# A float32 streaming-encoder block on one core: the down projection as seven block products, with weight sums formed by adding transfers

## The chip, the cores and the metric

The kernel runs on one core of one Trainium2 chip. A core has a matrix engine (TensorE, called PE in the profile, with its weight loads as PEld), three engines for elementwise work (VectorE or DVE, ScalarE or ACT, GpSimd or POOL), a queue engine that here only issues transfers (SyncE or SP), and 16 DMA engines that carry the transfers issued by SP, ACT and POOL. The engines run at the same time; each takes its own instructions in order, and an instruction waits for semaphores that others raise. The metric is the device time of one execution in microseconds; less is better.

## What is computed

One layer: 512 tokens of 1024 features, with 16 learned tokens put in front, go through two attention branches, a merge, a gated feed-forward part with a short convolution, and residual norms. All of it is float32. The change touches only the last product, the down projection, and what leads to it:

```python
hn = _rmsnorm(h, norm_ffn_pre[l])
up = hn @ w_ffn_up[l]
act = jax.nn.gelu(_causal_dwconv(up, conv_w[l], conv_b[l]), approximate=True)
ffn = (act * (hn @ w_ffn_gate[l])) @ w_ffn_down[l]
h = h + _rmsnorm(ffn, norm_ffn_post[l])
```

`w_ffn_down` is 2816 by 1024, and 512 tokens of the result are returned. So the last line multiplies a 512 by 2816 matrix with a 2816 by 1024 one, scales each token by its root mean square and a gain, and adds `h`.

## The kernel before, in words

**Products in three parts.** TensorE multiplies in a short format here (float32r). To keep float32 accuracy, each operand x is split into a high part, a copy cast to float32r, and a low part, x minus the high part. A product is the sum of three: high by high, high by low, low by high. A split is two instructions on two engines: a cast on ACT (line 88 in `load_w`, line 134 in `split`), and then a subtraction that reads the cast (line 89, on POOL for weights; line 135, on DVE for activations).

**The feed-forward loop** (lines 919 to 942) runs over `FT` = 22 blocks of 128 features. For each block `m` it loads 128 columns of the up and of the gate weights, multiplies them with the normed tokens (`pt_up`, 48 matmuls; `ga`, 24 matmuls), applies the convolution and GELU to the first product, multiplies the two, and splits the result into `fh` and `fl`, which stay in SBUF. The normed tokens are `h2h` and `h2l`; the residual `hb` stays in SBUF to the end.

**The down projection** (lines 945 to 1006) is in three column ranges. Columns 0 to 511: for each of 11 chunks of weights (two blocks of 128 rows by 512 columns, 512 KB) it loads, splits, and runs 24 matmuls of 512 columns, for four tiles of 128 tokens (`d01`, `d23`). Columns 512 to 767: six chunks, matmuls of 256 columns (`dq`). Columns 768 to 1023: all weights are loaded and split first (`raw_e`, `wdh`, `wdl`), then one token tile after the other is multiplied (`e`), so that the norm, the residual and the store of a tile run while the next tile is multiplied. In all this stage, 22 blocks by 4 token tiles by 3 products give 264 matmuls for each column range.

**What sets the order.** The program is written as above, and a scheduler places the instructions on each engine; within an engine the order is then fixed. SP carries all weight loads in one queue. Three `raw` buffers of 512 KB are shared by all weight loads, so a load waits until an earlier chunk has been split. The split chunks have two buffers in the pool `wp` (tags `wh`, `wl`).

Of the kernel before, what the change touches and what calls it, by code (L numbers as in the profile page):

```python
# [49 lines left out]
def block_kernel(ctx: ExitStack, tc: tile.TileContext, x, meta_tokens, norm_mix_pre, w_in, w_gk_up, b_gk,  # L50
# [155 lines left out]
    def diagonal(pl, r, n, nm):  # L206
        """r on the diagonal: a product with it transposes and scales by token."""
        d = pl.tile([P, P], F32, tag="dr", name=f"dr{nm}", bufs=2)
        dve.tensor_scalar(out=d[:n, :n], in0=ident[:n, :n], scalar1=r, scalar2=None, op0=ALU.mult)
        return d[:n, :n]  # L210

    with tc.tile_pool(name="p0", bufs=2, side="right") as p0:
        xts = {i: p0.tile([P, D], F32, name=f"xt{i}", bufs=1) for i in range(1, 5)}
# [115 lines left out]
    # =================== gated linear attention ===================  # L329
    with ExitStack() as pgs:  # L330
        pgc = pgs.enter_context(tc.tile_pool(name="pgc", bufs=1))
        # masks: level masks by compressed query, and the diagonal
# [248 lines left out]
    with tc.tile_pool(name="pa", bufs=1) as pa:  # L581

        def sb_parts(j, k, q, v):
            """Both parts of a head's keys stacked, against each part of its queries twice; values with both parts side by side."""
# [66 lines left out]
        def sb(j, ks, qh, ql, vs):  # L651
# [115 lines left out]
    # the last two meta tokens: too few for the array, their products are summed over the blocks of 128 rows first  # L767
# [36 lines left out]
    with tc.tile_pool(name="pw", bufs=1) as pw:  # L804
# [7 lines left out]
        def gained(i, pt, hf):  # L812
            """Half of the mixed output of a tile with the gain, and its sum of squares."""
# [12 lines left out]
        def normed(i):  # L826
            """Residual, second norm, and both parts of the result by feature."""
# [16 lines left out]
        def mini():  # L844
            """The same for the last two meta tokens, by feature from the start."""
# [30 lines left out]
        # the first half of the columns for all tokens, then the second one token tile at a time  # L876
# [38 lines left out]
        normed(4)  # L915
    p2.close()

    # =================== gated MLP with the causal convolution ===================
    pq = ctx.enter_context(tc.tile_pool(name="pq", bufs=1, side="right"))
    fh = pq.tile([P, FT, SEQ], F32R, name="fh")  # L920
    fl = pq.tile([P, FT, SEQ], F32R, name="fl")
    with tc.tile_pool(name="pu", bufs=2) as pu:
        for m in range(FT):
            pt = proj(load_w(cols(w_up, m * P), KT, f"up{m}", into=wx if m % 2 else None), h2h, h2l, FFNS, f"up{m}", apart=m < 2)
            y = pu.tile([P, SEQ], F32, tag="y", name=f"cy{m}")
# [14 lines left out]
            dve.tensor_tensor(out=y, in0=pg_, in1=y, op=ALU.mult)  # L940
            split(fh[:, m, :], fl[:, m, :], y)
# [4 lines left out]
    # =================== down projection, norm, residual ===================  # L946
    with tc.tile_pool(name="pd", bufs=1) as pd:
        QC = 256
        wdh = pd.tile([P, FT, QC], F32R, name="wdh")
        wdl = pd.tile([P, FT, QC], F32R, name="wdl")  # L950
        pos = [mmt("d01"), mmt("d23")]
        p4 = [pst(f"dq{i}", "sz"[i % 2]) for i in range(4)]
        ssq = pd.tile([P, 4, 3], F32, name="ssq")

        def down(c0, ncol, dsts):
            step = 1024 // ncol
            for k0 in range(0, FT, step):
                nk = min(step, FT - k0)
                wh, wl = load_w(w_down[k0 * P : (k0 + nk) * P, c0 : c0 + ncol].rearrange("(k p) m -> p k m", p=P), nk, f"d{c0}_{k0}")
                for kk in range(nk):  # L960
                    k = k0 + kk
                    for i in range(4):
                        t = slice(i * P, i * P + P)
                        for q, (a, b) in enumerate(((fh, wh), (fh, wl), (fl, wh))):
                            pe.matmul(dsts[i], a[:, k, t], b[:, kk, :], start=k == 0 and q == 0, stop=k == FT - 1 and q == 2)  # L965
# [3 lines left out]
        junk = pd.tile([P, 512], F32, name="dj")
        yb = pd.tile([P, 4, D], F32, name="yb")  # L970

        def gain3(i, src, c0):
            n = src.shape[-1]
            dve.tensor_tensor(out=yb[:, i, c0 : c0 + n], in0=src, in1=g3bc[:, c0 : c0 + n], op=ALU.mult)  # L974

        def square(i, src, q):
            act.activation(junk[:, : src.shape[-1]], src, AF.Square, accum_out=ssq[:, i, q : q + 1])  # L977
# [54 lines left out]
```

## Time and profile before

| | us |
|---|---|
| median of 3 runs (981.71 to 983.47) | 981.96 |
| span of the profiled execution | 983.2 |
| TensorE busy in it | 958.5 (97%) |
| down projection, three column ranges on TensorE | 61.60, 31.23, 31.25 |
| from the end of the last matmul (976.92) to the end of the span | 6.28 |

The span is the time from the first to the last instruction of one execution under the profiler; that execution lies 1.2 us above the median of the runs. The median is the number that a change is measured by. TensorE's granted clock is 0.990 over the span.

The page's first part gives the busy time of each engine, its second part the same in 40 slices of 24.6 us. The chain of waits leads back from the last instruction to whatever released each step. A table of windows gives the busy time of each engine in chosen stretches, with the share of the 16 DMA engines in use and the bytes they moved. The groups by line give a mean time for each kind of instruction. A busy TensorE is not by itself a bound; whether anything on it waits is read from the chain and from the idle time before its groups.

### The profile page before, as it was taken

How to read it: one execution, taken by the hardware profiler on the slowest of the kernel's cores; microseconds unless marked ns; L12 is line 12 of the kernel's file. 1: busy time of each engine (PE TensorE's matmuls, PEld its weight loads, DVE VectorE, ACT ScalarE, POOL GpSimd, SP SyncE). 2: the span in 40 equal slices, each digit the busy share in tenths (PEclk: the TensorE clock that was granted, in tenths of full speed). 3: DMA queues.
4: the chain of work that ended last, by engine and by line, in shares of the span. 5: the costliest groups of instructions: out<-in, count | busy, mean ns of one | idle time of the engine just before them, and what ended most of it. 6: DMA issues, size and time to landing. Idle time of an engine off the chain costs nothing.

```text
span 983.2 us, 17022 instructions
## 1 busy us (share of the span) xinstructions
PE 958.5 (97%) x6918; PEld 895.8 (91%) x6918; DVE 558.8 (57%) x970; ACT 461.5 (47%) x868; POOL 401.2 (41%) x285
## 2 busy tenths in 40 slices
PE   7999999999999998999999899999999999999997
PEld 7999999999999998999998779999988999888997
DVE  6675867767547786787849957444343444300112
ACT  5664645545467574676663244533333333311331
POOL 5523232222244454454545433543443443243460
PEclk9999999999999999999999899999999999999999
DMA  7122221222222222222223441333323323223231
GB/s 212 45 65 65 65 55 54 65 66 60 67 58 72 71 65 65 65 65 66 72 58 112 153 144 43 100 95 91 103 86 92 102 86 95 78 86 102 82 117 65
DMA packets 127552, 81.28 MB, mean 83 GB/s; under 512 B 3680, under 2 KB 120162, under 8 KB 127474
## 3 DMA queue, kind: packets, MB, share of 16 engines
q1 hardware_dynamic: 126082, 76.00, 27.0%
q10 hardware_dynamic: 1392, 4.19, 1.1%
q8 instruction: 54, 0.88, 0.4%
q14 instruction: 24, 0.20, 0.1%
HBM read 78.09 MB, written 2.10 MB: 82 GB/s over the span
## 4 chain that ended last, share of the span: by engine, by line
PE 85%; DVE 8%; issue 2%; ACT 2%; POOL 1%; DMA 1%; SPq 1%; DVEq 0%; POOLq 0%; ACTq 0%
PE pt_up L109 13%; PE ga L938 12%; PE d L965 6%; PE pt_gr L109 5%; PE pt_gv L109 5%; PE pt_go L109 4%; PE pt_mg L109 4%; PE e L998 3%; PE dq L965 3%; PE pt_gk L109 2%; PE pt_sv L109 2%; PE wo L887 2%; PE pt_ms L109 2%; PE pt_gq L109 2%; PE pt_sk L109 2%
## 5 line engine op out<-in xcount | busy, mean ns | idle before, releaser
L89 POOL TENSOR_TENSOR wl_up<-raw_up,wh_up 128x1024 fp32r<-128x1024 f32 x22 | 52.9, 2406 | 70.8 <-ACT wh_up L88 70.8
L89 POOL TENSOR_TENSOR wl_ga<-raw_ga,wh_ga 128x1024 fp32r<-128x1024 f32 x22 | 52.6, 2393 | 56.6 <-ACT wh_ga L88 56.6
L929 DVE SCALAR_TENSOR_TENSOR cy<-pt_up,cw,cy 128x511 f32<-128x511 f32 (+1 forms) x44 | 32.8, 746 | 74.1 <-ACT cy L926 74.1
L109 PE MATMUL pt_up<-h2l,wh_up 128*128 128x256 f32 (+1 forms) x352 | 73.6, 283 | 0.3 <-DVE h2l L204 0.2
L109 PE MATMUL pt_up<-h2h,wh_up 128*128 128x256 f32 (+1 forms) x352 | 73.5, 283 | 0.0
L109 PE MATMUL pt_up<-h2h,wl_up 128*128 128x256 f32 (+1 forms) x352 | 73.3, 282 | 0.0
L938 PE MATMUL ga<-h2l,wh_ga 128*128 128x512 f32 (+1 forms) x192 | 72.2, 376 | 0.0
L938 PE MATMUL ga<-h2h,wl_ga 128*128 128x512 f32 (+1 forms) x192 | 72.1, 375 | 0.0
L938 PE MATMUL ga<-h2h,wh_ga 128*128 128x512 f32 (+1 forms) x192 | 72.1, 376 | 0.0
L89 POOL TENSOR_TENSOR wl_d<-raw_d,wh_d 128x1024 fp32r<-128x1024 f32 (+1 forms) x17 | 39.6, 2332 | 63.7 <-ACT wh_d L88 63.7
L88 ACT CAST wh_up<-raw_up 128x1024 fp32r<-128x1024 f32 x22 | 23.0, 1050 | 85.6 <-PE pt_up L109 76.2
L135 DVE TENSOR_TENSOR fl<-cy,fh 128x512 fp32r<-128x512 f32 x22 | 50.2, 2282 | 15.1 <-ACT fh L134 15.1
L109 PEld LDWEIGHTS pt_up<-h2h,wh_up 128*128 128x128 f32 x352 | 56.9, 189 | 1.7
L109 PEld LDWEIGHTS pt_up<-h2l,wh_up 128*128 128x128 f32 x352 | 55.5, 189 | 0.7 <-DVE h2l L204 0.7
L109 PEld LDWEIGHTS pt_up<-h2h,wl_up 128*128 128x128 f32 x352 | 55.4, 189 | 0.0
L88 ACT CAST wh_d<-raw_d 128x1024 fp32r<-128x1024 f32 (+1 forms) x17 | 17.5, 1029 | 65.8 <-PE d L965 45.1
L940 DVE TENSOR_TENSOR cy<-ga,cy 128x512 f32<-128x512 f32 x22 | 15.2, 691 | 49.0 <-PE ga L938 47.9
L938 PEld LDWEIGHTS ga<-h2h,wl_ga 128*128 128x128 f32 x192 | 36.2, 188 | 7.0
L938 PEld LDWEIGHTS ga<-h2l,wh_ga 128*128 128x128 f32 x192 | 36.2, 188 | 6.2
L938 PEld LDWEIGHTS ga<-h2h,wh_ga 128*128 128x128 f32 x192 | 36.2, 188 | 6.1
L974 DVE TENSOR_TENSOR yb<-d,g3bc 128x512 f32<-128x512 f32 x4 | 2.8, 692 | 61.3 <-ACT dj L977 61.2
L965 PE MATMUL d<-wl_d,fh 128*128 128x512 f32 x88 | 34.8, 396 | 0.0
(522 smaller groups left out, 3234.4 us busy)
## 6 DMA issues: line engine op xcount, KB each, us to landing
raw_up<-in_w_ffn_up_dram SPq DMA_DIRECT2D x22, 512.0 KB, 4.0
raw_ga<-in_w_ffn_gate_dram SPq DMA_DIRECT2D x22, 512.0 KB, 3.9
raw_d<-in_w_ffn_down_dram SPq DMA_DIRECT2D x16, 512.0 KB, 3.5
raw_gv<-in_w_in_dram SPq DMA_DIRECT2D x8, 512.0 KB, 3.9
raw_gr<-in_w_in_dram SPq DMA_DIRECT2D x8, 512.0 KB, 3.8
raw_mg<-in_w_in_dram SPq DMA_DIRECT2D x8, 512.0 KB, 3.9
raw_go<-in_w_gla_out_dram SPq DMA_DIRECT2D x8, 512.0 KB, 4.1
raw_ms<-in_w_in_dram SPq DMA_DIRECT2D x8, 512.0 KB, 3.9
```

Of the source, the lines that this page charges most:

```text
L88: act.copy(hi_out, raw)
L89: lo_eng.tensor_tensor(out=lo_out, in0=raw, in1=f32(hi_out), op=ALU.subtract)
L109: pe.matmul(dst, a[:, k, :], b[:, k, lo:hi], start=n == 0, stop=n == len(steps) - 1)
L135: dve.tensor_tensor(out=lo, in0=src, in1=f32(hi), op=ALU.subtract)
L887: pe.matmul(d0[i], m[k][:, t], w, start=k == 0 and q == 0, stop=k == 7 and q == 2)
L929: dve.scalar_tensor_tensor(out=y[:, d:], in0=pt[:, : SEQ - d], scalar=c, in1=y[:, d:], op0=ALU.mult, op1=ALU.add)
L938: pe.matmul(pg_[:, lo:hi], a[:, k, :], b[:, k, lo:hi], start=lo == 0 and k == 0 and q == 0, stop=k == KT - 1 and q == 2, skip_group_check= ...
L940: dve.tensor_tensor(out=y, in0=pg_, in1=y, op=ALU.mult)
L965: pe.matmul(dsts[i], a[:, k, t], b[:, kk, :], start=k == 0 and q == 0, stop=k == FT - 1 and q == 2)
L974: dve.tensor_tensor(out=yb[:, i, c0 : c0 + n], in0=src, in1=g3bc[:, c0 : c0 + n], op=ALU.mult)
L998: pe.matmul(dst, a[:, k, t], b[:, k, :], start=k == 0 and q == 0, stop=k == FT - 1 and q == 2)
```

## The change

The 512 by 2816 by 1024 product is cut into halves three ways: the tokens into two halves of 256, the 1024 columns into `L` and `R`, and the 22 feature blocks into the even (11) and the odd (11) ones. That gives eight block products in the plain way. The changed kernel forms seven (Strassen's scheme in Winograd's form, with signs turned so that the weight sums only add):

- Of the activations it needs four sums besides the blocks `A11`, `A12`, `A22`: `S1`, `S2`, `S3`, `S4`. They are formed on DVE in the feed-forward loop, once for each pair of blocks, on 256 tokens. `A11` and `S1` are split there at once (`Ah`, `Al`); the other five stay whole in `As` and are split again chunk by chunk when their product runs (`sh`, `sl`).
- Of the weights it needs four sums besides the blocks, in the two buffers `tw` and `tv`, 2.9 MB each. T1 (both halves of the even rows) is loaded into `tw` by SP, and the other half is added by transfers issued on POOL with `accum_op=ALU.add`: the transfer reads what lies in SBUF, adds the weights from DRAM, and writes the sum back. T2 adds a third block to `tw` on DVE (line 1035). T4 adds a fourth to `tw` by adding transfers again (line 1079). T3 adds one to `tv` by adding transfers (line 1090).
- The products run in the order p1, p5, p6, p2, p3, p7, p4. Each has 11 blocks by 2 token tiles by 3 products = 66 matmuls of 512 columns. A product's chunk of weights is 512 KB as before; the last chunk has half of that. All splits of weights are now a cast on ACT and a subtraction on DVE; POOL has none in this stage.
- The accumulators are added up on DVE, ACT and in PSUM (p2 runs on top of p1, p3 on top of p5, p7 on top of p6).
- `hb` is written to DRAM before the feed-forward loop (line 919, issued by ACT) and read back into `hbr` (line 1084, issued by SP).

The core of the diff:

```diff
+        for i in range(4):
+            act.dma_start(hbd[i], hb[:, i, :])
...
+            p = m // 2
+            dve.tensor_tensor(out=yp[:, 2, :], in0=yp[:, 1, :], in1=As[:, A22, p, :], op=ALU.subtract)
+            split(Ah[:, :, p, :], Al[:, :, p, :], yp[:, 0:3:2, :])
+            dve.tensor_tensor(out=As[:, S3, p, :], in0=yp[:, 0, :], in1=yp[:, 1, :], op=ALU.subtract)
+            dve.tensor_tensor(out=As[:, S2, p, :], in0=yp[:, 2, :], in1=yp[:, 0, :], op=ALU.subtract)
+            dve.tensor_tensor(out=As[:, S4, p, :], in0=As[:, S2, p, :], in1=As[:, A12, p, :], op=ALU.add)
...
+        def product(nm, operand, source, dsts, first, last):
+            for n, (q, nk) in enumerate(CH):
+                src = source(q, nk)
+                pl_ = pd if turn[0] % 2 else wp
+                turn[0] += 1
+                wh = pl_.tile([P, nk, HC], F32R, tag="wh", name=f"wh_{nm}{q}", bufs=2)
+                wl = pl_.tile([P, nk, HC], F32R, tag="wl", name=f"wl_{nm}{q}", bufs=2)
+                split(wh, wl, src)
+                ah, al = operand(q, nk, nm)
...
+                        pe.matmul(dsts[i], a[:, kk, t], b[:, kk, :], start=first and q + kk == 0 and j == 0,
+                                  stop=last and q + kk == NP - 1 and j == 2, skip_group_check=True)
...
+            def of(q, nk):
+                r = raw_of(s, c, q, nk, nm)
+                t = tw[:, q : q + nk, :]
+                dve.tensor_tensor(out=t, in0=t, in1=r, op=ALU.add)
+                return t
...
+        product("p1", whole(A11), plain(0, L, "p1"), qa, True, True)
+        for q, nk in CH:
+            sp.dma_start(tw[:, q : q + nk, :], block(0, L, q, nk))
+            pool.dma_start(out=tw[:, q : q + nk, :], in_=block(0, R, q, nk), accum_op=ALU.add)
...
+        product("p5", whole(S1), lambda q, nk: tw[:, q : q + nk, :], qd, True, True)
...
+        product("p6", late_split(S2), summed(1, R, "t2"), qb, True, True)
...
+        for q, nk in CH:
+            pool.dma_start(out=tw[:, q : q + nk, :], in_=block(1, L, q, nk), accum_op=ALU.add)
+        product("p2", late_split(A12), plain(1, L, "p2"), qa, False, True)
+        for q, nk in CH:
+            sp.dma_start(tv[:, q : q + nk, :], block(1, R, q, nk))
+        for i in range(4):
+            sp.dma_start(hbr[:, i, :], hbd[i])
...
+        product("p3", late_split(S4), lambda q, nk: tv[:, q : q + nk, :], qd, False, True)
+        for q, nk in CH:
+            pool.dma_start(out=tv[:, q : q + nk, :], in_=block(0, R, q, nk), accum_op=ALU.add)
...
+        product("p7", late_split(S3), lambda q, nk: tv[:, q : q + nk, :], qb, False, True)
...
+        product("p4", late_split(A22), lambda q, nk: tw[:, q : q + nk, :], qe, True, True)
```

Three places of the fixed order are spoken of later. In the names, `p12` is product p1's chunk that begins at block 2 of its 11, `t22` the chunk of the third weight block that is added into `tw` from block 2 on, and so on; the number after the last underscore only tells buffers apart.

On ACT, at the passage from the feed-forward loop to the down projection, the casts of the weight chunks stood before as:

```order
L143 ACT_TABLE_LOAD
L134 CAST fh_7341<-cy21_9465 128x512
L968 DMA g3bc_9522<-in_norm_ffn_post_dram 128x1024
L88 CAST wh_d0_4_9588<-raw_d0_4_9586 128x1024
L88 CAST wh_d0_6_9618<-raw_d0_6_9616 128x1024
```

and stand now as:

```order
L143 ACT_TABLE_LOAD
L134 CAST Ah_7352<-yp20_9400 128x2x256
L134 CAST wh_p18_9629<-raw_p18_9627 128x1024
L984 DMA g3bc_9550<-in_norm_ffn_post_dram 128x1024
L134 CAST wh_p12_9575<-raw_p12_9573 128x1024
L134 CAST wh_p16_9611<-raw_p16_9609 128x1024
```

The chunks were cast in the order of their use; now the cast of chunk 8 stands ahead of the cast of chunk 2, while TensorE still takes the chunks as 0, 2, 4, 6, 8. Chunks 0, 4 and 8 take turns in the two `wh` buffers of `wp`, so chunk 8 gets the buffer that chunk 0's matmuls leave.

On DVE, in p5 (its low parts are `wl_p50`, `wl_p52` and so on), the additions that form T2 for p6 stand between the subtractions that p5 needs; before, DVE had no weight work:

```order
L135 TENSOR_TENSOR wl_p50_9674<-tw_9547,wh_p50_9673 128x1024
L1035 TENSOR_TENSOR tw_9547<-tw_9547,raw_t20_9772 128x1024
L135 TENSOR_TENSOR wl_p52_9690<-tw_9547,wh_p52_9689 128x1024
L135 TENSOR_TENSOR wl_p54_9706<-tw_9547,wh_p54_9705 128x1024
L1035 TENSOR_TENSOR tw_9547<-tw_9547,raw_t22_9795 128x1024
```

So p5's second chunk comes behind the first addition, and that behind the load of `raw_t20`.

On SP, from the loads of p2's first chunks to the end, the queue was and is (first the end of the queue before, then the one now):

```order
L83 DMA raw_e16_10188<-in_w_ffn_down_dram 128x4x256
L83 DMA raw_e20_10192<-in_w_ffn_down_dram 128x2x256
L1006 DMA out_0_dram<-yb_9525 128x512 x4
```

```order
L992 DMA raw_p20_9912<-in_w_ffn_down_dram 128x2x512
L992 DMA raw_p22_9934<-in_w_ffn_down_dram 128x2x512
L992 DMA raw_p24_9956<-in_w_ffn_down_dram 128x2x512
L1082 DMA tv_9769<-in_w_ffn_down_dram 128x2x512 x5
L1082 DMA tv_9769<-in_w_ffn_down_dram 128x512
L1084 DMA hbr_9770<-hbd_6816 128x1024 x4
L992 DMA raw_p26_9978<-in_w_ffn_down_dram 128x2x512
L992 DMA raw_p28_10000<-in_w_ffn_down_dram 128x2x512
```

The second half of p2's own weights stands behind all of `tv` and behind the residual `hbr`. `tv` and `hbr` lie where `Ah` and `Al` lay, which p5 reads to its last matmul.

More of the change, by code (lines that the diff above doesn't have):

```diff
@@ L944, in block_kernel @@
     p3.close()
[L947 to L965, printed above, removed]
+    with tc.tile_pool(name="pd", bufs=1, reuse_waits="tile") as pd:
+        wd = w_down.rearrange("(q s p) m -> s p q m", s=2, p=P)
+        HC = D // 2
+        CH = [(q, min(2, NP - q)) for q in range(0, NP, 2)]
+        tw = pd.tile([P, NP, HC], F32, name="tw")
+        p1 = pd.tile([P, 2, HC], F32, name="p1")
+        yb = pd.tile([P, 4, D], F32, name="yb")
@@ L967, in block_kernel @@
         g3bc = pd.tile([P, D], F32, name="g3bc")
+        junk = pd.tile([P, HC], F32, name="dj")
+        ssq = pd.tile([P, 4, 2], F32, name="ssq")
         act.dma_start(g3bc, norm_ffn_post[0].partition_broadcast(P))
[L969 to L977, printed above, removed]
@@ L992, in block_kernel, with block @@
-        pl = [mmt("e0"), pst("e1"), mmt("e2"), pst("e3", "z")]
-        for i in range(4):
-            dst = pl[i][:, :QC]
-            t = slice(i * P, i * P + P)
-            for k in range(FT):
-                for q, (a, b) in enumerate(((fh, wdh), (fh, wdl), (fl, wdh))):
-                    pe.matmul(dst, a[:, k, t], b[:, k, :], start=k == 0 and q == 0, stop=k == FT - 1 and q == 2)
-            square(i, dst, 2)
+        L, R = slice(0, HC), slice(HC, D)
+        def block(s, c, q, nk):
+            return wd[s][:, q : q + nk, c]
@@ new lines, in summed, with halves, square, gain @@
+        def summed(s, c, nm):
+            def of(q, nk):
[3 more added lines that the diff above has]
+                return t
+            return of
+        def halves(t):
+            return [t[:, i * HC : i * HC + HC] for i in range(2)]
+        def square(i, src, h):
+            act.activation(junk, src, AF.Square, accum_out=ssq[:, i, h : h + 1])
+        def gain(i, src, c):
+            dve.tensor_tensor(out=yb[:, i, c], in0=src, in1=g3bc[:, c], op=ALU.mult)
@@ new lines, in block_kernel @@
+        for i in range(2):
+            act.copy(yb[:, 2 + i, R], qd[i])
+        pqa.close()
+        pt = ctx.enter_context(tc.tile_pool(name="pt", bufs=1, side="right", reuse_waits="tile"))
+        tv = pt.tile([P, NP, HC], F32, name="tv")
+        hbr = pt.tile([P, 4, D], F32, name="hbr")
+        qb = halves(mmt("dB"))
+        product("p6", late_split(S2), summed(1, R, "t2"), qb, True, True)
+        for i in range(2):
+            dve.tensor_tensor(out=yb[:, i, R], in0=qb[i], in1=p1[:, i, :], op=ALU.add)
@@ new lines, in block_kernel @@
+        for q, nk in CH:
+            pool.dma_start(out=tv[:, q : q + nk, :], in_=block(0, R, q, nk), accum_op=ALU.add)
+        for i in range(2):
+            dve.tensor_tensor(out=yb[:, i, R], in0=qd[i], in1=yb[:, i, R], op=ALU.subtract)
+            square(i, yb[:, i, R], 1)
+            finish(i, R, yb[:, i, R])
+        product("p7", late_split(S3), lambda q, nk: tv[:, q : q + nk, :], qb, False, True)
+        for i in range(2):
+            o = yb[:, 2 + i]
+            dve.tensor_tensor(out=o[:, L], in0=qb[i], in1=p1[:, i, :], op=ALU.add)
+            dve.tensor_tensor(out=o[:, R], in0=o[:, R], in1=o[:, L], op=ALU.subtract)
+            square(2 + i, o[:, R], 1)
+            gain(2 + i, o[:, R], R)
@@ L1009 @@
+        qe = [pst("dE0"), pst("dE1", "z")]
+        product("p4", late_split(A22), lambda q, nk: tw[:, q : q + nk, :], qe, True, True)
+        for i in range(2):
+            o = yb[:, 2 + i, L]
+            dve.tensor_tensor(out=o, in0=qe[i], in1=o, op=ALU.add)
+            square(2 + i, o, 0)
+            finish(2 + i, L, o)
 _INS = ["x", "meta_tokens", "norm_mix_pre", "w_in", "w_gk_up", "b_gk", "gla_head_norm", "w_sb_out", "w_gla_out", "w_o",
```

79 lines of the change are left out of this document (56 added, 23 removed).

## The prediction

> **What bounds the kernel now.** I read the chain of waits first, from the end of the feed-forward loop on (start, length, what):
>
> ```profile
> 841.52 5.76 PE pt_up L109 x48
> 847.28 5.56 PE ga L938 x24
> 852.84 61.60 PE d L965 x264
> 914.44 31.23 PE dq L965 x264
> 945.67 31.25 PE e L998 x264
> 976.92 0.02 issue
> ...
> 978.71 0.75 DVE yb L1005
> 979.47 0.66 DVEq L1028
> ```
>
> The whole down projection is one unbroken run of TensorE, 61.60 + 31.23 + 31.25 = 124.1 us, and then a tail. Second, the windows for these four stretches, for what else is in use there:
>
> ```profile
> core 0: us, PE busy (x) PEld busy (x) DVE busy (x) ACT busy (x) POOL busy (x), PEclk, DMA share, GB/s
> 852.84:914.44 61.60, 61.60 (x267) 49.59 (x266) 1.97 (x3) 11.86 (x13) 23.95 (x10) 1.00 0.29 89
> 914.44:945.67 31.23, 31.23 (x267) 31.23 (x266) 2.61 (x5) 11.38 (x17) 18.77 (x9) 1.00 0.40 121
> 945.67:976.92 31.25, 31.24 (x265) 31.04 (x263) 8.46 (x24) 5.81 (x20) 5.29 (x3) 1.00 0.16 60
> 976.92:983.20 6.28, 0.00 (x0) 0.00 (x0) 2.39 (x7) 0.97 (x4) 0.00 (x0) 0.75 0.22 84
> ```
>
> TensorE is full at granted clock 1.00. DVE is almost idle, ACT has 11.86 of 61.60, and the DMA engines are used to 16 to 40%. So the stage is bound by TensorE alone, and the change trades TensorE time against DVE and DMA time. Whether there is room for the latter decides.
>
> **TensorE: -16.3.** 61.60 / 264 = 233.3 ns for a matmul of 512 columns (31.23 / 264 = 118.3 ns for 256). Seven products of 66 matmuls are 462 x 233.3 ns = 107.8, 15.4 a product, 2.80 a chunk of 12. 107.8 - 124.1 = -16.3.
>
> **Prices of the split.** These are from groups by line and single instructions:
>
> ```profile
> L929 DVE SCALAR_TENSOR_TENSOR cy<-pt_up,cw,cy 128x511 f32<-128x511 f32 (+1 forms) x44 | 32.8, 746 | 74.1 <-ACT cy L926 74.1
> L89 POOL TENSOR_TENSOR wl_d<-raw_d,wh_d 128x1024 fp32r<-128x1024 f32 x15 | 35.9, 2396 | 59.8 <-ACT wh_d L88 59.8
> L88 ACT CAST wh_d<-raw_d 128x1024 fp32r<-128x1024 f32 x15 | 15.8, 1054 | 58.4 <-PE d L965 45.1 <-PE dq L965 9.3 <-issue 2.6
> L1005 DVE SCALAR_TENSOR_TENSOR yb<-yb,a_out,hb 128x512 f32<-128x512 f32 x8 | 5.7, 748 | 0.1
> L974 DVE TENSOR_TENSOR yb<-d,g3bc 128x512 f32<-128x512 f32 x4 | 2.8, 692 | 61.3 <-ACT dj L977 61.2
> L974 DVE TENSOR_TENSOR yb<-e,g3bc 128x256 f32<-128x256 f32 x4 | 1.7, 416 | 0.0
> L134 ACT CAST fh<-cy 128x512 fp32r<-128x512 f32 x2 | 1.2, 622 | 1.9 <-DVE cy L940 1.9
> 842.50 2.39 POOL L89 TENSOR_TENSOR wl_d<-raw_d,wh_d 128x1024 fp32r<-128x1024 f32 x1 [3.17 <-ACT wh_d L88]
> 843.01 2.43 DVE L135 TENSOR_TENSOR fl<-cy,fh 128x512 fp32r<-128x512 f32 x1 [0.69 <-ACT fh L134]
> 854.33 0.69 DVE L135 TENSOR_TENSOR fl<-cy,fh 128x512 fp32r<-128x512 f32 x1 [0.69 <-ACT fh L134]
> 979.50 0.34 ACTq L1006 DMA_DIRECT2D out_dram<-yb  x1
> ```
>
> A DVE instruction with both inputs in SBUF takes 0.69 for 512 elements alone and 2.43 when POOL's subtraction runs beside it. In the new stage POOL computes nothing, so I take 0.69, and from 0.42 for 256 and 0.69 for 512 the estimate for 1024 is 0.69 + 2 x 0.27 = 1.23. A chunk then costs ACT 1.05 + 0.62 = 1.67 and DVE 1.23 + 0.69 = 1.92, both under TensorE's 2.80. The steady state holds.
>
> **Feed-forward loop: +0.4.** For a pair of blocks DVE loses one 512 subtraction and gains four of 256. Even if each of the four were held up for 2.4, a pair has about 5.2 in convolutions and gating products (4 x 0.75, 2 x 0.69, the rest small ones), 4 x (0.42 + 2.4) and a 2.43, some 19 of the 2 x 11.32 (5.76 + 5.56) that TensorE needs; accumulators are double, so nothing waits. If that cover were gone, the excess would show 11 times. The four stores of `hb` cost ACT 0.34 each; one stands on the way to the first product (+0.4; 0 to 1.4).
>
> **Entry, +3.5.** ACT reaches chunk 8's cast after the last feed-forward block and waits there for a buffer that p1's chunk 0 leaves at 2.80 after the loop's end. Then 1.05, the 0.34 of the `g3bc` issue, and 1.05 for chunk 2's cast: 5.24, and 1.23 more until its low part, 6.47. TensorE has chunk 2 due at 2.80: it waits 2.44, runs 0.23, waits 1.0. Sum 3.4 and a few semaphores; 2.4 at least, as the cast alone is that late.
>
> **The transfers.** Rows: one plain load, the saturated DMA engines, and two queues at once.
>
> ```profile
> raw_d<-in_w_ffn_down_dram SPq DMA_DIRECT2D x16, 512.0 KB, 3.5
> out_dram<-yb SPq DMA_DIRECT2D x4, 256.0 KB, 2.0
> 3.00:4.00 1.00, 1.00 (x7) 1.00 (x6) 0.00 (x0) 0.00 (x0) 1.00 (x4) 1.00 1.00 369
> 564.00:566.00 2.00, 2.00 (x10) 1.60 (x10) 2.00 (x4) 1.35 (x3) 1.26 (x1) 1.00 1.02 418
> 944.00:945.00 1.00, 1.00 (x11) 1.00 (x10) 0.00 (x0) 1.00 (x2) 0.58 (x2) 1.00 1.00 338
> ```
>
> At a full share the 16 engines move 338 to 418 GB/s. I take 369: a chunk of 524,288 bytes holds them 1.42 us, and from issue to landing there is some 2 us besides (3.5 - 1.42). No row shows an adding transfer. It holds the engines at least for one copy (1.42; its bytes must come from DRAM, which excludes less), at most for three (read, read, write each at a copy's price, 4.26). I take two, 2.84: two reads, with the write under them as in a copy, whose own read and write fit in one 1.42. That is nearest to the plain copy by one read.
>
> By the Trainium skill's "Collectives: The Full Stack", section "The bandwidth ceiling", an add in the DMA engines needs two source reads on one ring and runs at half the rate of a copy, 32.35 GB/s against 62.28. By it an adding chunk is estimated at 2.84 (by the measured ratio, 1.93 times a copy, 2.74) and the sum below would stay within 1 us; no run here shows it yet.
>
> *In p5, +5.6.* DVE's second subtraction of p5 stands behind the first T2 addition, which waits for `raw_t20`. On SP's queue that load is the seventh chunk from the loop's end (5.5 of `tw`, 0.5 of p1, itself); ACT's `g3bc` is an eighth, and about four adding chunks take turns with them: 8 + 4 x 2 = 16 x 1.42 = 22.7, with 2.3 around (0.3 until SP issues, the 2 us besides), landing at 25.0; addition and subtraction end at 27.5. TensorE is due there at 15.4 + 3.5 + 2.80 + 0.23 = 21.9. So +5.6. With adding chunks at one copy, 12 x 1.42: 21.8, nothing; at three, +11.3.
>
> *In p2, +12.6.* After p5's last matmul SP has these chunks in line: two of p2, 5.5 of `tv`, four of `hbr` (512 KB each), then p2's chunk 6: 12.5 in all. POOL's 5.5 adding chunks for T4 become free in the same time, as p6's splits read `tw`. 12.5 + 5.5 x 2 = 23.5 x 1.42 = 33.4, and 1 around, as the queue is running already: 34.4, then a cast of 1.05 and, after a first matmul, 1.0 for the low part. TensorE is due 15.4 (p6) + 3 x 2.80 = 23.8 after p5. +12.6. At one copy it is 18 x 1.42, +4.8; at three, +20.4. Even with transfers at no time it is +2.7: ACT has chunk 8's activation cast, which needs the buffer of chunk 4, ahead of chunk 6's weight cast (0.62 + 1.05 + 1.0).
>
> **Last products, +2.0.** p7 and p4 have 11 weight chunks' splits, 2 x 5.5 x 1.92 = 21.1 on DVE, and the finish of two token tiles, the additions for the other two, their gains: 10 x 0.69, 4 x 0.75 and some 1.2 of small ones, 11. 32.2 against 30.8 of TensorE, unevenly spread: I take 2 (0 to 4).
>
> **Tail, +3.4.** Both last token tiles now end together. DVE's 2.39 of the old tail, with a gain of 0.69 for 0.42, is 2.66 a tile; two, and two additions of 0.69, are 6.7; then 0.34 of issue, 2.0 to landing and about 0.6 of waits: 9.7 in place of 6.28.
>
> **Sum:** -16.3 + 0.4 + 3.5 + 5.6 + 12.6 + 2.0 + 3.4 = +11.2. Against its own profiled execution (983.2) that is 994.4; that execution was 1.2 above the runs' median, so 993.2, said as **993**.
>
> **Rivals.** *Adding costs what copying costs:* p5's stall goes, p2's is 4.8: -16.3 + 0.4 + 3.5 + 4.8 + 2.0 + 3.4 = -2.2, 980; at 350 GB/s instead, about 982. For it: a copy already reads and writes at once. Against it: a second read has to go somewhere. *Adding costs three copies:* p5 +11.3, p2 +20.4, in all +24.7, 1007. For it: nothing shows that the write overlaps; POOL also has to write the descriptors itself. *The other side, faster:* the two queues fill each other's gaps, as in the row of 418, so that the plain loads never wait for the adding ones; p5 is free, p2 at its 2.7: -16.3 + 0.4 + 3.5 + 2.7 + 2.0 + 3.4 = -4.3, 977.7. For it is that 418 row, and that the stage's DMA share was only 0.16 to 0.40. It decides where p2's chunk 6 lands within 22 of p5's end. Against it: the stage's bytes, 12.5 plain chunks alone, are already 17.8 of that.
>
> One more sentence from the Trainium skill: "DMA: Bandwidth & Descriptors", section "Issuing engines are not separate DMA queues", says that transfers issued by SP, ACT and GpSimd run on the same 16 engines and interleave, which speaks against this last rival. The 418 row is no more than a short peak.
>
> **How the numbers follow.** Forecast (two copies) 0.47; three copies 0.23; one copy 0.17; faster 0.13. A difference under 0.2% (2 us) can't be told from none. The one-copy case lies at the border, so I give it as 0.05 faster, 0.08 same, 0.04 slower. Faster 0.13 + 0.05 = 0.18, same 0.08, slower 0.47 + 0.23 + 0.04 = 0.74. The range is from 980, the one-copy case, to 1009, a little over three copies: it leaves out most of the 0.13 and about 0.05 above. The forecast's own range, by 338 to 418 GB/s, is 986 to 998.
>
> **What would show it.** Right: 462 matmuls in p1 to p7 at 233 ns each; TensorE idle in p1 before chunk 2, 3 to 4 us, released by ACT and DVE; in p5 the line 1035 addition waiting for `raw_t`; in p2 a cast of `raw_p2` waiting for its transfer for about 10; DMA share near 1.0 in p1, p5, p6 and the first half of p2. Wrong: a DMA share well under 1 while TensorE waits, or `tw` landing 4 us after issue (then it is not the engines that are short), or waits of TensorE in p3 and p7, where the adding transfers have time, or `ga` and `pt_up` slower than 5.56 and 5.76 each.

## The result and the profile after

| | us |
|---|---|
| before, median of 4 runs (981.71 to 985.46) | 982.72 |
| after, median of 4 runs (993.67 to 995.31) | 994.12 |
| ratio, with its 95% interval | 1.0105 (1.0074 to 1.0135) |
| span of the profiled execution after | 991.7 |

The changed kernel is slower by 11.4 us, about 1.05%. The forecast was 993.

The chain of waits of the changed kernel, from the end of the feed-forward loop on (start, length, what):

```profile
845.22 5.56 PE ga L957 x24
850.79 2.81 PE dA L1013 x12
...
863.00 17.92 DMA raw_t<-in_w_ffn_down_dram
...
892.08 19.10 DMA tv<-in_w_ffn_down_dram
...
911.24 13.12 DMA raw_p<-in_w_ffn_down_dram
...
924.38 1.05 ACT wh_p L134
925.46 1.24 DVE wl_p L135
926.74 9.25 PE dA L1013 x29
935.99 15.28 PE dD L1013 x66
951.27 15.49 PE dB L1013 x66
966.76 15.06 PE dE L1013 x65
```

Before, this part of the chain was TensorE without a break. Now, after p1's first chunk, TensorE stands in it only for the last 29 matmuls of p2 and for p3, p7 and p4. Ahead of these it runs through transfers: T2's third block, then the third block of `tv`, then p2's chunk 6, which stands behind all of `tv` on SP's queue. SP issued chunk 6's load only at 911.24, when that block of `tv` had landed (892.08 + 19.10). Its own waits from 884 to 926 (in all, times, longest) show that the last three of p2's loads each waited for a landing of `tv`; what ties the one to the other was not followed up:

```profile
SPq L992 <- DMA tv<-in_w_ffn_down_dram: 7.2, 3, 3.6
```

The windows of the changed kernel, one from each product's first matmul to that of the next (p1, p5, p6, p2, p3, p7, p4) and the tail. After the two times come busy time and count on PE, PEld, DVE, ACT and POOL, then the granted clock, the DMA share and GB/s:

```profile
850.63:870.81 20.18, 17.16 (x67) 13.34 (x66) 9.19 (x12) 6.27 (x8) 7.14 (x6) 0.92 0.99 273
870.81:888.42 17.61, 15.93 (x67) 12.17 (x66) 11.51 (x11) 8.85 (x11) 0.00 (x0) 1.00 0.89 227
888.42:903.71 15.29, 15.29 (x68) 12.40 (x67) 12.20 (x14) 8.87 (x13) 7.01 (x6) 1.00 1.01 250
903.71:935.83 32.12, 18.52 (x67) 14.03 (x66) 11.63 (x14) 8.94 (x13) 2.41 (x2) 0.73 0.80 231
935.83:951.11 15.28, 15.28 (x67) 12.40 (x66) 11.54 (x15) 9.86 (x17) 4.51 (x4) 1.00 0.93 156
951.11:966.60 15.49, 15.49 (x68) 12.32 (x66) 15.32 (x28) 10.72 (x21) 0.00 (x0) 1.00 0.09 35
966.60:981.64 15.04, 15.04 (x66) 12.21 (x65) 10.77 (x16) 6.61 (x13) 0.00 (x0) 1.00 0.09 35
981.64:991.70 10.06, 0.39 (x2) 0.00 (x0) 6.43 (x16) 2.33 (x8) 0.00 (x0) 0.73 0.28 105
```

Four products take what TensorE needs, 15.0 to 15.5. Three are too long: p1 by 4.9, p5 by 2.3, p2 by 16.8 (each against the 15.28 of p3). In p1, p5 and p6 the DMA share is 0.89 to 1.01, yet only 227 to 273 GB/s are moved, where the plain loads of the row of 369 before filled it. In p1 and p2 the granted clock is 0.92 and 0.73.

TensorE's matmuls at these two places, from the timeline (start, length; in brackets the idle time before and who ended it):

```profile
855.67 0.50 PE L1013 MATMUL dA<-wh_p,Ah 128*128 128x512 f32 x1 [2.08 <-ACT wh_p L134]
857.12 0.80 PE L1013 MATMUL dA<-wl_p,Ah 128*128 128x512 f32 x1 [0.94 <-DVE wl_p L135]
857.71 0.63 PE L1013 MATMUL dA<-wh_p,Al 128*128 128x512 f32 x1
858.14 0.63 PE L1013 MATMUL dA<-wh_p,Ah 128*128 128x512 f32 x1
...
925.48 0.79 PE L1013 MATMUL dA<-wh_p,sh_p 128*128 128x512 f32 x1 [13.13 <-ACT wh_p L134]
926.74 0.79 PE L1013 MATMUL dA<-wl_p,sh_p 128*128 128x512 f32 x1 [0.47 <-DVE wl_p L135]
```

The waits are where they were forecast: 2.08 + 0.94 ahead of p1's second chunk, 13.13 + 0.47 ahead of p2's chunk 6. Behind each, matmuls follow at 0.43 (857.71 to 858.14) and not at 0.233. One microsecond of p1, from a window:

```profile
858.00:859.00 1.00, 1.00 (x4) 0.71 (x4) 1.00 (x3) 0.00 (x0) 1.00 (x1) 0.50 1.02 221
```

The granted clock is 0.50 there. It stays so for some 3 us in p1, and in p2 until 931.6.

The queues in the stretch from 850 to 992 (packets, MB, share of the 16 engines):

```profile
q0 software_dynamic: 4512, 8.65, 34.4%
q1 hardware_dynamic: 7312, 14.94, 30.0%
```

POOL's queue, that of the adding transfers, holds the engines longer for 8.65 MB than SP's (q1) for 14.94. The packets of the two are of much the same size, 1.9 and 2.0 KB in the mean (8.65 MB / 4512 and 14.94 MB / 7312), but one took 0.173 us in the first and 0.093 in the second (34.4% and 30.0% of 16 engines' 142 us, over the counts).

### The profile page after: what moved, and what is told of

It is laid out like the page before. It is cut to its first block, busy times and chain, and to the rows that moved or that the text cites. A ratio compares the mean times of both kernels' runs of the same rounds, so it can differ in the third digit from the quotient of the medians.

```text
span 991.7 us, 16616 instructions
## 1 busy us (share of the span) xinstructions
PE 945.0 (95%) x6588; PEld 870.0 (88%) x6588; DVE 631.5 (64%) x1087; ACT 487.5 (49%) x902; POOL 367.5 (37%) x280
## 3 DMA queue, kind: packets, MB, share of 16 engines
q0 software_dynamic: 4512, 8.65, 4.9%
q10 hardware_dynamic: 1968, 6.29, 1.8%
## 4 chain that ended last, share of the span: by engine, by line
PE 74%; DVE 12%; DMA 7%; issue 2%; ACT 2%; POOL 1%; SPq 0%; DVEq 0%; ACTq 0%; POOLq 0%
PE pt_up L109 13%; PE ga L957 12%; PE pt_gr L109 5%; PE pt_gv L109 5%; PE pt_mg L109 4%; PE pt_go L109 4%; DVE acc L776 3%; PE pt_ms L109 3%; PE pt_gk L109 2%; PE pt_sv L109 2%; DMA raw_t<-in_w_ffn_down_dram 2%; PE pt_gq L109 2%; DMA tv<-in_w_ffn_down_dram 2%; DMA raw_p<-in_w_ffn_down_dram 2%; PE pt_sk L109 2%
## 5 line engine op out<-in xcount | busy, mean ns | idle before, releaser
L89 POOL TENSOR_TENSOR wl_ga<-raw_ga,wh_ga 128x1024 fp32r<-128x1024 f32 x22 | 55.1, 2507 | 57.4 <-ACT wh_ga L88 57.4
L948 DVE SCALAR_TENSOR_TENSOR cy<-pt_up,cw,cy 128x511 f32<-128x511 f32 (+1 forms) x22 | 16.4, 746 | 60.8 <-ACT cy L945 60.8
L88 ACT CAST wh_ga<-raw_ga 128x1024 fp32r<-128x1024 f32 x22 | 22.9, 1047 | 25.9 <-PE ga L957 25.5
L948 DVE SCALAR_TENSOR_TENSOR yp<-pt_up,cw,yp 128x511 f32<-128x511 f32 (+1 forms) x22 | 16.4, 745 | 27.5 <-ACT yp L945 27.5
L134 ACT CAST sh_p<-As 128x512 fp32r<-128x512 f32 (+1 forms) x30 | 17.4, 584 | 32.6 <-PE dA L1013 11.3
L89 POOL TENSOR_TENSOR wl_gr<-raw_gr,wh_gr 128x1024 fp32r<-128x1024 f32 x8 | 19.0, 2372 | 35.9 <-ACT wh_gr L88 33.1
L89 POOL TENSOR_TENSOR wl_gv<-raw_gv,wh_gv 128x1024 fp32r<-128x1024 f32 x7 | 16.9, 2416 | 38.0 <-ACT wh_gv L88 38.0
L135 DVE TENSOR_TENSOR sl_p<-As,sh_p 128x512 fp32r<-128x512 f32 (+1 forms) x30 | 19.2, 643 | 13.7 <-ACT sh_p L134 13.7
```

The source lines that it names most:

```text
L88: act.copy(hi_out, raw)
L89: lo_eng.tensor_tensor(out=lo_out, in0=raw, in1=f32(hi_out), op=ALU.subtract)
L134: act.copy(hi, src)
L135: dve.tensor_tensor(out=lo, in0=src, in1=f32(hi), op=ALU.subtract)
L948: dve.scalar_tensor_tensor(out=y[:, d:], in0=pt[:, : SEQ - d], scalar=c, in1=y[:, d:], op0=ALU.mult, op1=ALU.add)
```

## The experiments

All times are set against runs of the kernel before on the same chip. The products of all kernels, in us from first matmul to first matmul (in the last two kernels the borders overlap by a few matmuls), in the changed kernel's order; x7 runs p2 second:

| | p1 | p5 | p6 | p2 | p3 | p7 | p4 | tail | ratio to before (95%) |
|---|---|---|---|---|---|---|---|---|---|
| after | 20.18 | 17.61 | 15.29 | 32.12 | 15.28 | 15.49 | 15.04 | 10.06 | 1.0105 (1.0074 to 1.0135) |
| x1 plain transfers | 18.86 | 16.21 | 15.28 | 20.41 | 15.28 | 15.47 | 15.05 | 10.08 | 0.9972 (0.9953 to 0.9991) |
| x2 p2's loads first | 20.43 | 16.87 | 15.28 | 17.92 | 15.28 | 15.48 | 15.03 | 10.11 | 0.9972 (0.9958 to 0.9985) |
| x3 T4 late | 20.41 | 17.31 | 15.28 | 17.42 | 15.27 | 15.47 | 15.06 | 10.50 | 0.9979 (0.9961 to 0.9997) |
| x4 entry | 17.06 | 22.66 | 15.27 | 30.71 | 15.27 | 15.43 | 15.02 | 10.06 | 1.0103 (1.0083 to 1.0123) |
| x5 both | 20.42 | 17.23 | 15.28 | 15.41 | 15.28 | 15.46 | 15.03 | 10.57 | 0.9950 (0.9931 to 0.9969) |
| x6 warm | 18.84 | 24.61 | 15.28 | 27.52 | 15.28 | 15.50 | 15.05 | 10.06 | 1.0088 (1.0061 to 1.0115) |
| x7 p2 second | 15.64 | 15.68 | 15.99 | 16.42 | 15.38 | 15.68 | 15.26 | 9.09 | 0.9895 (0.9874 to 0.9917) |
| x8 p2 in its old place | 15.27 | 24.70 | 15.02 | 15.38 | 15.27 | 15.43 | 15.26 | 9.02 | 0.9962 (0.9946 to 0.9979) |

### What an adding transfer costs (x1)

```diff
-            pool.dma_start(out=tw[:, q : q + nk, :], in_=block(0, R, q, nk), accum_op=ALU.add)
+            pool.dma_start(out=tw[:, q : q + nk, :], in_=block(0, R, q, nk))
```

The same at lines 1079 and 1090.

> The 17 adding transfers become plain ones that overwrite; order on every engine stays as it is. Left out: the weight sums T1, T3 and T4 are not formed, so p5, p7 and p4 multiply a single block. Theory (an adding transfer holds the DMA engines like two copies, and p2 waits because they are full): the share of POOL's queue in the stage falls from about 34% to about 17%; p5 falls from 17.6 to 15.4 to 16; p2's load of chunk 6 has 18 chunks of 1.42 in front and lands 26.6 after p5's end against 23.8 due: p2 falls from 32.1 to 20 to 23, total 981 to 985. Rival (the order of SP's queue alone, whatever a transfer costs): p2 stays above 28, total 989 or more. Rival (adding costs what copying costs): POOL's share and the time do not move, 992 to 996.

Measured: 979.62 us beside 983.08 before. POOL's queue in the stage of this kernel:

```profile
q0 software_dynamic: 2400, 8.65, 19.7%
```

And TensorE's waits in p2, from its timeline:

```profile
910.08 0.50 PE L1013 MATMUL dA<-wh_p,sh_p 128*128 128x512 f32 x1 [2.12 <-ACT wh_p L134]
911.34 0.76 PE L1013 MATMUL dA<-wl_p,sh_p 128*128 128x512 f32 x1 [0.76 <-DVE wl_p L135]
```

The same bytes on the same queue take 19.7% of a stage of 126 us, where the adding ones took 34.4% of one of 142: 24.8 against 48.8 us of all 16 engines. The price is what makes the changed kernel slow: without it p2's wait falls from 13.6 to 2.9, and the kernel is a little faster than before. It is not all: with plain transfers p2 still loses 5.1. The total came out a little under the theory's 981 to 985. The plain packets on this queue are twice as large (2400 for the same 8.65 MB), but that is not the difference: SP's plain packets, as small as the adding ones, took 0.093 beside 0.173 in the changed kernel. What the engines do in the longer time of an adding packet, a second read, as the prediction had it, or something else, no run shows.

### The order of SP's queue, and T4's time (x2, x3, x5)

x2, where `last_raw` is the last load of p2's own chunks:

```diff
+        with tc.issue_after(last_raw[0].ins):
             for q, nk in CH:
                 sp.dma_start(tv[:, q : q + nk, :], block(1, R, q, nk))
             for i in range(4):
                 sp.dma_start(hbr[:, i, :], hbd[i])
```

> p2's own loads ahead of tv and hbr on SP's queue; T4's adding transfers stay where they are. Theory (chunk 6 is late because 9.5 plain chunks stand in front of it on a full queue): p2 takes 15.4 to 17, tv's first chunk has 17.5 chunk prices of 1.42 in front and lands 25 after p5's end against 30.7 due for p3, so no later product waits; the total falls by 15 to 17, to 977 to 979. Rival (the adding transfers beside them are the cause, whatever the order): a plain chunk lands only every 1.42 + 2.84 = 4.3 while T4 is added, against 2.8 that TensorE takes, so p2 still loses 4 to 6, 982 to 985.

x3, where `last_t3` is the last of T3's adding transfers:

```diff
-        for q, nk in CH:
-            pool.dma_start(out=tw[:, q : q + nk, :], in_=block(1, L, q, nk), accum_op=ALU.add)
...
+        with tc.issue_after(last_t3.ins):
+            for q, nk in CH:
+                pool.dma_start(out=tw[:, q : q + nk, :], in_=block(1, L, q, nk), accum_op=ALU.add)
```

> T4's adding transfers behind T3's on POOL's queue, so that none runs in p6 and p2; SP's queue stays as it is. Theory (the engines' time is what p2 lacks): 12.5 plain chunks of 1.42 land p2's chunk 6 at 18.8 after p5's end against 23.8 due, p2 takes 15.4 to 18; T4's 5.5 chunks of 2.84 then fill p7, and p4 starts 0 to 3 late; total 977 to 982. Rival (the order on SP and the wait of tv for the buffers of Ah and Al make chunk 6 late by themselves): p2 stays above 24, total above 986.

x5 has both edits.

> Both edits of the two runs before together: p2's loads ahead of tv and hbr, and T4's adding transfers behind T3's. Theory (each edit alone left p2 a rest of 2.6 and 2.1, the one because T4 is added beside p2's loads, the other because tv and hbr stand in front of them): p2 falls to 15.3 to 16, the stage to 124 to 125 from the first matmul to the end, total 977.5 to 979.5. Rival (the rest is the order of ACT and DVE in p2, not transfers): p2 stays at 17 to 18, 980 to 981.

Measured: 980.31 (x2) and 981.13 (x3) beside 983.08 before, and 977.43 beside 983.03 with both (x5). The window of p2 in x2:

```profile
903.48:921.40 17.92, 16.44 (x67) 12.01 (x66) 11.36 (x14) 8.68 (x13) 2.41 (x2) 1.00 1.07 341
```

In x3:

```profile
907.08:924.50 17.42, 15.97 (x68) 12.16 (x67) 11.45 (x14) 8.68 (x13) 2.41 (x2) 1.00 0.52 173
```

In x5:

```profile
903.75:919.16 15.41, 15.41 (x67) 12.31 (x66) 11.45 (x14) 8.69 (x13) 2.41 (x2) 1.00 0.83 308
```

Each edit alone takes nearly all of p2's 16.8 away, so the wait needs both: plain chunks in front of chunk 6, and adding transfers that share the engines with them. x3 came out as its theory said; x2 lies between its theory (p2 at 15.4 to 17) and its rival (a loss of 4 to 6). What each leaves, 2.6 and 2.1, goes when the other joins it, as the theory of x5 said. Both single edits let the scheduler move some splits on ACT and DVE in p2 as well; that this order was not the rest is shown by x5's 15.41 in the order of x2.

The same bytes are moved in all four. In x3, T4's adding transfers run in p7, where nothing else moves. The window of three microseconds there:

```profile
941.00:944.00 3.00, 3.00 (x15) 2.42 (x14) 3.00 (x6) 2.97 (x7) 0.00 (x0) 1.00 1.12 199
```

And the queues in it, of which there is only POOL's:

```profile
q0 software_dynamic: 312, 0.60, 111.8%
```

With the engines full and no other queue, adding transfers move 199 GB/s (195 to 209 in stretches of 2 us of p7). A chunk of 524,288 bytes takes 2.63. That is 1.85 times the 1.42 of a plain one. By the Trainium skill's "Collectives: The Full Stack", section "The bandwidth ceiling", the ratio of copying to adding was 1.93 in rings of four ranks, and the page limits its model to rings of three or more. This run's 1.85 lies within 5% of it, for an add into SBUF on one core.

### The entry (x4)

```diff
-                pl_ = pd if turn[0] % 2 else wp
+                pl_ = pd if turn[0] // 2 % 2 else wp
```

> The split buffers taken in pairs from the two pools, so that p1's second chunk is cast inside the feed-forward loop, as its first is. Theory (the entry costs what it was given, 3.5 of waiting and 1.8 of lower granted clock behind it): p1 falls from 20.2 to 15.4 to 16.5 and the total by 4 to 5, to 989 to 990. Rival (p1 and p5 together are held by the DMA engines, which are full from the loop's end on, so a stall removed in p1 comes back in p5): p1 falls as much, p5 rises from 17.6 to 20 to 22, total within 1.5 of the changed kernel, 993 to 995.

Measured: 993.13 beside 983.08 before. The windows of p1 and p5:

```profile
851.02:868.08 17.06, 15.72 (x67) 12.13 (x65) 7.98 (x12) 6.33 (x9) 5.35 (x5) 1.00 0.98 271
868.08:890.74 22.66, 18.51 (x66) 14.11 (x67) 14.47 (x14) 8.89 (x11) 1.79 (x2) 0.85 0.91 235
```

T2's first addition, from DVE's timeline:

```profile
873.74 1.23 DVE L1035 TENSOR_TENSOR tw<-tw,raw_t 128x1024 f32<-128x1024 f32 x1 [4.46 <-DMA raw_t<-in_w_ffn_down_dram]
```

And p5's second chunk, from TensorE's:

```profile
876.16 0.79 PE L1013 MATMUL dD<-wl_p,Ah 128*128 128x512 f32 x1 [3.61 <-DVE wl_p L135]
```

The rival was right. p1 gains 3.1, p5 gives back 5.1 (its clock also falls, to 0.85), p2 gains 1.4, and the total moves by less than the two intervals can tell apart. TensorE now reaches p5's second chunk earlier, but T2's first addition, which stands ahead of its subtraction on DVE, begins 22.7 after p1's first matmul (873.74 - 851.02), as in the changed kernel (22.4). The wait in p1 was real, and yet worth nothing: `raw_t20` landed no sooner.

### The clock behind a wait (x6)

```diff
+                for k in range({("p1", 1): 9, ("p2", 3): 54}.get((nm, n), 0)):
+                    with tc.issue_after(mm.ins):
+                        mm = pe.matmul(idle[:, :P], ident, ident, start=True, stop=True)
```

> The changed kernel with matmuls of the identity put where TensorE waits: 9 (about 2.0) ahead of p1's second chunk, 54 (about 12) ahead of p2's fourth; nothing else. Theory (after a wait TensorE's granted clock is 0.50 for some microseconds, which cost 1.8 in p1 and 3.0 in p2): the clock stays at 1.00, p2 falls from 32.1 to 29 to 29.7; p1 from 20.2 to 18.4 to 19, most of which p5 gives back because the DMA engines are full; total falls by 2.5 to 4.5, to 990 to 991.5. Rival (the matmuls behind a wait are slow because of the transfers beside them, not for having waited): p1 and p2 keep their length, 993.5 to 995.

Measured: 992.56 beside 983.03 before, with the widest spread of all (990.07 to 997.48). The profiled execution is the longest of the five, so the lengths below are not those of the median. The windows of p1, p5 and p2:

```profile
853.36:872.20 18.84, 17.81 (x85) 14.46 (x84) 9.07 (x12) 6.17 (x8) 5.02 (x4) 1.00 0.98 266
872.20:896.81 24.61, 18.32 (x68) 14.42 (x66) 14.19 (x15) 9.16 (x11) 4.17 (x4) 0.79 0.86 211
...
912.09:939.61 27.52, 27.52 (x175) 24.37 (x174) 11.64 (x14) 8.86 (x13) 2.41 (x2) 1.00 0.78 235
```

Where TensorE was kept busy the granted clock stayed at 1.00, and the matmuls behind the wait came at 0.233 again. So the slow matmuls come from having waited, not from the transfers beside them. The sizes were missed. p2 fell by 4.6, more than the 3 of the clock, for two reasons of opposite sign: p5 had grown, so the transfers had more time and chunk 6 landed 32.1 after p5's end (928.88 - 896.81) where it had been 35.9; but the inserted matmuls ran to 932.57, 2.6 beyond the end of chunk 6's cast (929.94). p5 grew by 7.0, more than p1's 1.3: T2's first addition began 26.1 after p1's first matmul (879.50 - 853.36, where the changed kernel has 22.4), TensorE waited 6.29 for it, and the clock fell behind that wait (0.79). The scheduler had also moved one T2 addition on DVE. The total says nothing about the clock, then; the windows do.

### A version that beats both (x7), and what makes it so (x8)

The core of x7's edit: p2 is the second product, and each of its loads from the third on has a chunk of T1 behind it, while T1's first two chunks follow p1's loads (`t1_sum` is T1's chunk, with T2's addition two chunks behind). Beside it, T4 stands behind T3; all splits and T2's additions are held in the order of use on ACT and DVE; the buffers come in pairs, as in x4; p1's accumulators are two tiles of one bank each; and in p1 and p4 the last two chunks are multiplied token tile by token tile.

```diff
+        def t1(q, nk, behind):
+            with tc.issue_after(loads[behind]):
+                sp.dma_start(tw[:, q : q + nk, :], block(0, L, q, nk))
             pool.dma_start(out=tw[:, q : q + nk, :], in_=block(0, R, q, nk), accum_op=ALU.add)
+
+        def plain_t1(q, nk):
+            r = raw_of(1, L, q, nk, "p2")
+            if q // 2 + 0 < len(CH) and q // 2 + 0 >= 2:
+                t1(*CH[q // 2 + 0], ("p2", q))
+            return r
...
+        product("p2", late_split(A12), plain_t1, qa, False, True, ready)
...
+        product("p5", whole(S1), t1_sum, qd, True, True)
```

> The same seven products, with p2 moved between p1 and p5, T1's loads and adding transfers spread between p2's loads, T4's behind T3's, the splits kept in the order of use, p1's second chunk split inside the loop, and in p4 the last two chunks token tile by token tile. Theory (the stage's transfers are 16.5 plain and 16.5 adding chunks beside hbr's 4, at 1.42 and 2.56 some 71 of 108 us of TensorE: there is room if no product is asked for its sums too early): p1, p5, p6, p3, p7, p4 take 15.0 to 16 each, p2 15.5 to 18, the tail 8.5 to 9.5, sum 118 to 122 against 130.4 before; total 8 to 12 less than the kernel before, ratio 0.988 to 0.992. Rival (p1 and p2 together still ask for more than the engines move: 13.5 plain and 5.5 adding chunks in 31): p2 takes 20 or more, ratio 0.994 or above.

Measured: 972.1 beside 983.03 before, ratio 0.9895 (0.9874 to 0.9917). The windows of p1, p2, p5, p6, p3, p7, p4 and the tail:

```profile
852.06:867.70 15.64, 15.43 (x68) 12.21 (x66) 7.88 (x10) 6.29 (x9) 2.61 (x2) 1.00 0.92 251
867.70:884.12 16.42, 16.29 (x67) 12.24 (x67) 10.03 (x13) 9.71 (x14) 4.33 (x4) 1.00 1.03 301
884.12:899.80 15.68, 14.92 (x64) 11.52 (x63) 12.78 (x14) 8.19 (x13) 0.17 (x1) 1.00 0.80 223
...
962.11:971.20 9.09, 0.17 (x1) 0.00 (x0) 5.40 (x14) 1.56 (x6) 0.00 (x0) 0.65 0.31 115
```

No product loses more than 1.1, the clock is 1.00 in all seven, and the stage takes 119.1 where it took 130.4 before. x8 has the same edits with p2 back behind p6; T1's loads then all follow p1's, `tv` and `hbr` follow p2's, and p1's accumulators are one tile again:

> The kernel of the run before with p2 back in its old place behind p6 (p2's loads still ahead of tv and hbr); T1's loads then follow p1's, two of them ahead of p1's last. Theory (the place of p2 is what gives T1 and T2 the time to arrive): p1 15.4 to 16, but p5 has p1's and its own 30.8 of TensorE for 2.5 + 5.5 + 5.5 plain chunks and 5.5 adding ones, 13.5 x 1.42 + 5.5 x 2.56 = 33.3, and its second chunk stands behind T2's first addition: p5 20 to 24, ratio 0.994 to 0.999. Rival (the order of the splits, the entry and the last product made the gain, not the place): p5 15.4 to 17, ratio 0.988 to 0.992 as in the run before.

Measured: 978.54 beside 982.62 before. The window of p5:

```profile
866.02:890.72 24.70, 18.36 (x69) 13.12 (x68) 13.19 (x13) 10.03 (x13) 3.33 (x3) 0.93 0.94 245
```

And TensorE's longest wait in it:

```profile
879.62 0.80 PE L1034 MATMUL dD<-wl_p,Ah 128*128 128x512 f32 x1 [4.30 <-DVE wl_p L134]
```

p5 is at 24.7, a little over the theory's range, and no other product differs from x7 by more than 1.1. The place of p2, which needs no sum, ahead of p5, which needs one, is worth 0.67% (0.9962 against 0.9895, the intervals do not touch), and the loss lies in p5. The other edits of x7 were not tried one by one; x8, which has them and x5's two, is no faster than x5 (0.9962 against 0.9950).

## Why the prediction was right, point by point

The forecast was right in its sign, its size and its mechanism: TensorE's gain is eaten by waits for transfers, most of all in p2. Its terms were less exact than their sum: p1, p2 and the tail were too small by 5.8 in all, p5 and the last products too large by 5.3, and TensorE's gain too small by 0.8. That the sum came within 1 us is luck. All against the same two profiled executions:

| term | predicted | measured | from |
|---|---|---|---|
| TensorE's work | -16.3 | -17.1 | 7 x 15.28, against 124.1 |
| feed-forward loop | +0.4 | +0.3 | the rows below |
| entry, p1 | +3.5 | +4.9 | waits 3.02, the rest the clock |
| p5 | +5.6 | +2.3 | waits 1.68, the cause of the rest is open |
| p2 | +12.6 | +16.8 | waits 13.60, the rest the clock |
| p3, p7, p4 | +2.0 | 0.0 | 45.81, against 3 x 15.28 |
| tail | +3.4 | +3.6 | 991.70 - 981.82 = 9.88, against 6.28 |
| sum | +11.2 | +10.8 | |

The first third of the up products (count; shortest, median and longest ns; first and last start; forms), of the kernel before:

```profile
L109 PE MATMUL pt_up<-h2h,wh_up x352: 276/282/385, 598.4 to 846.5; 128*128 128x256 f32 x168, 128*128 128x258 f32 x8
```

Of the changed kernel:

```profile
L109 PE MATMUL pt_up<-h2h,wh_up x352: 276/282/386, 596.1 to 844.5; 128*128 128x256 f32 x168, 128*128 128x258 f32 x8
```

The loop takes 248.4 in place of 248.1. It began 2.3 earlier in this execution, so the spans differ by 8.5 only. I do not count that as an effect of the change: in x1 to x8, with the same code ahead of the loop, p1's first matmul started anywhere from 848.96 to 854.08, and the medians differ by 11.4.

**The price of the adding transfer** was taken as 2.84 between bounds of 1.42 and 4.26; it is 2.63. This was the choice that decided, and x1 shows that with one copy's price the sign would have turned, as the rival had it (0.9972; the rival said 980, 0.998).

**p2** was right in place and cause (x2, x3). Chunk 6 was to land 34.4 after p5's end and landed 35.9 after it (924.36 - 888.42). The count of what was in front was short. SP's queue in this stretch, and in the next one, from 924.36 to 928:

```profile
q1 hardware_dynamic: 3510, 7.75, 60.0%
...
q1 hardware_dynamic: 53, 0.08, 5.8%
```

These 7.75 MB are 14.8 chunks, where I had counted 12.5. One of the 2.3 is p2's first load: it was issued at 887.16, but moved no more than 0.04 MB before p5's end, so three of p2's loads stood in line and not two. The other 1.3 are of chunks 8 and 10, which stand behind chunk 6 in the queue and were still served beside it: when it landed, only 0.08 MB of their 1.5 chunks was left. 14.8 x 1.42 + 5.5 x 2.63 = 35.5.

**p5** was oversized. The load was to land 25.0 after the loop's end. The addition that waits for it, on DVE:

```profile
872.99 1.22 DVE L1035 TENSOR_TENSOR tw<-tw,raw_t 128x1024 f32<-128x1024 f32 x1 [5.14 <-DMA raw_t<-in_w_ffn_down_dram]
```

And TensorE behind it:

```profile
875.40 0.50 PE L1013 MATMUL dD<-wl_p,Ah 128*128 128x512 f32 x1 [1.16 <-DVE wl_p L135]
```

It began at 22.2 (872.99 - 850.79): by then POOL's queue had moved 1.65 MB, 3.1 adding chunks where four had been counted, and each of them was cheaper than 2.84. TensorE came 1.5 later than thought (875.40 - 1.16 - 850.79 = 23.4 for 21.9), mostly because p1 was longer. Both make the wait shorter: 1.16, and 0.52 more in a later chunk. x6, where it began 3.7 later, shows that this landing is not fixed. So the term was right in its kind and uncertain by some 4 us.

**The term that was missing** is the clock behind a wait: 1.9 in p1 and 3.2 in p2, 5.1 in all, which x6 took away. The prediction had a granted clock of 0.75 in its own row of the old tail, behind TensorE's last matmul, and did not ask what a wait in mid-stage would do. By the Trainium skill's "TensorE: Matmul & The Clock Gate", section "What's actually happening", TensorE falls to half its clock after an idle window of about 3.4 us, and the window runs freely. The trace agrees in the half clock: it was granted at 0.50, with 0.43 for a matmul in place of 0.233. It fits a window that runs freely, too: waits of 2.08 and 0.94 cost the clock in the changed kernel, x2, x3 and x5, but not in x1, where the same two waits left it at 1.00. The length of 3.4 us no run here shows; neither of the two waits ahead of p1's slow matmuls is as long as that.

**The last products' +2.0** was not there: DVE's 15.3 of work in p7 fit under TensorE's 15.49. The entry's waits (3.02 for 3.4) and the tail came out as worked out. But the entry's term was no cost of its own, as adding the terms up supposed: x4 shows that p1 and p5 share one bound, the transfers.

**The rivals.** Three copies and one copy fell with the 2.63. The last, that the queues fill each other's gaps, fell with this window of p5, in which both queues were busy, and its two queues:

```profile
872.00:880.00 8.00, 6.84 (x30) 5.25 (x29) 5.41 (x5) 3.12 (x4) 0.00 (x0) 1.00 1.10 262
...
q0 software_dynamic: 543, 1.05, 70.5%
q1 hardware_dynamic: 544, 1.05, 39.5%
```

Both moved the same. A plain and an adding chunk, 1,048,576 bytes at 262 GB/s, took 4.0: 1.42 + 2.63, and nothing was filled.

## What to carry to other kernels

Work that is moved from an engine to a transfer is still paid, in engine-time of the DMA: an adding transfer is worth about 1.85 plain ones here, and the sum over a whole stage says nothing as long as a product early in it asks for its share at once. Check each queue for loads that are due sooner than what stands in front of them (with that and a later T4 the loss of 1.05% became a gain of 0.5%), and put the work that needs no sum where the sums are being made (x7, with this, gained 1.05%; the place alone brought 0.67%). A wait of TensorE is to be priced with the half clock behind it (1.9 behind waits of 3.02 in p1, 3.2 behind 13.60 in p2), and a wait that is removed is worth nothing while the next product waits for the same transfers.

## What was not expected of the hardware

- Behind waits of 3 us TensorE's matmuls took 0.43 in place of 0.233 for some 3 us, in four of five kernels with the same waits; behind 13.6 us of waiting for some 4 to 6 us (927.33 or 925.48 to 931.60).
- Loads that stand behind one another in one queue are served together: when p2's chunk 6 landed, 14.8 chunks had been moved since p5's end, 1.3 of them from the two loads behind it, and chunk 8 was there 1.3 us later.
- At a full share the engines moved 262 GB/s when half of the bytes were added, 199 when all were, and 385 when none were (p6 of x1, two queues), so GB/s at a full share tells how much of the traffic is adding.
